# A 512x2048 by 2048x2048 product in seven block products instead of eight, at the end of a two-layer kernel

## The chip, the core and the metric

The kernel runs on one core of a Trainium2 chip. A core has a matrix engine (TensorE, PE in the profile), an elementwise engine (VectorE, DVE), an activation engine (ScalarE, ACT), a general engine (GpSimd, POOL) and a queue for transfers (SyncE, SP); ACT and POOL issue transfers too. Each engine works off its own list of instructions in order, and waits at an instruction until the semaphores it names have come. The metric is the device time of one execution in microseconds, lower is better. The kernel before took 2392.82 us, the median of three runs from 2391.46 to 2393.68 us.

## The reference

Two transformer-like layers on 512 tokens of width 2048, in float32. Only the end of the second layer matters here: `x` is 512x2048, `w_ple_gate` is 2048x2048, and `p @ w_ple` has long been computed and stored.

```python
x = x + merged @ w_out
x = x + jax.nn.sigmoid(x @ w_ple_gate) * (p @ w_ple)
return rms_norm_2(x, final_g)          # x * rsqrt(mean(x*x) + 1e-6) * final_g, by token
```

## The kernel before

**One stream of weights.** The whole kernel is one list, `spine`, of units. A unit is a block of weights of 512 KB (128 partitions by 1024 numbers, in the last group 256 KB) and the matmuls that use it. Float32 accuracy comes from three matmuls in the `fp32r` type: a value is split into `hi` (the value rounded to fp32r) and `lo` (the rest), and `mm3` adds hi*hi, hi*lo and lo*hi in PSUM. So every block of weights is loaded (`wraw`, SP's queue), copied by ACT to `whi` and subtracted by DVE to `wlo`; this is `split`. Buffers of these three kinds share a pool of NW = 10.

**The order of the work.** Nothing is scheduled later: the order in which `emit` writes instructions is the order on every engine. The loop at the end of `emit` takes unit after unit. Between the matmuls of unit i it calls `ahead`, which writes the loads up to unit i+4 (LD) and the splits up to unit i+3 (LS), and `sides.pump`, which writes steps of side work (`Sides`, generators that yield what they wait for) as far as the clocks of a simple model of the engines allow. What is needed at once is forced: `ahead(True)` splits the unit's own weights, and `sides.until` and `drain` run side work to a condition.

**The stage of the change.** `out2` (`ch_units("w_out_2", ...)`) makes the 16 row blocks of x transposed, 128 channels by 512 tokens each: 48 matmuls a block, then `after_o2` adds the old x and splits the sum into `x2h` and `x2l`, and `x2_gen` transposes it on PE (tile `px2`) and stores it by token (`x2t`). Then comes the gate product, in five column groups (`GATES`): three of 512 columns and two of 256. In a group of 512 columns a unit holds two of the 16 k blocks; its 24 matmuls serve four token blocks b of 128 tokens, in four PSUM banks. After the last unit of a group `after_gate` works on each token block: ACT takes tanh from PSUM, DVE does two `scalar_tensor_tensor` with the stored p @ w_ple (`plel`) and x (`x3`), ACT squares and sums, DVE multiplies by `final_g`. The last group keeps all its weights (`whole_units`) and runs token block by token block, each followed by `finish`: the mean square, an inverse square root by Newton steps of one column (`rsqrt1`), scaling and the store of 128 rows in four transfers.

## Time and profile before

| | us |
|---|---|
| runs (3) | 2391.46, 2392.82, 2393.68 |
| profiled execution | 2393.15 |
| its span, first to last instruction | 2391.4 |
| first matmul of the gate product | 2202.84 |
| last matmul of the gate product ends | about 2379.5 |
| TensorE busy in the span | 2360.1 |
| VectorE, ScalarE, GpSimd busy | 1478.4, 929.6, 251.1 |
| granted TensorE clock, mean | 0.999 |

The profile is one execution, and the prediction's rows are counted from its span's start. The busy time of PE is that of pipelined matmuls whose bars overlap: a 512-column matmul shows as 0.39 us, and one starts every 0.23 us. A row of the timeline gives the start, the time, the engine, the line of the kernel and `output<-inputs`, and in brackets the idle time before it and what ended it.

### The profile page before, as it was taken

The page shows a single profiled execution, that of the slowest core. Times are in us where ns is not written, and L with a number is a line of the kernel's source. Part 1 is how long each engine was busy: PE and PEld are TensorE (multiplying, and loading weights), DVE is VectorE, ACT ScalarE, POOL GpSimd, SP SyncE. Part 2 cuts the span into 40 slices and gives each one's busy share as a digit, 9 for nine tenths or more (in the row PEclk, how much of TensorE's full clock was granted, in tenths as well). Part 3 has the DMA queues.
Part 4 walks back from the last instruction along what each step waited for, and adds up shares of the span by engine and source line. Part 5 has one row for each costly group of instructions (what it writes and reads, how often), then busy time and mean ns, then how long its engine had stood idle before and what let it go on. Part 6 is the DMA issues. An engine that isn't in the chain of part 4 may idle for free.

```text
span 2391.4 us, 31046 instructions
## 1 busy us (share of the span) xinstructions
PE 2360.1 (99%) x11587; PEld 1985.0 (83%) x11587; DVE 1478.4 (62%) x2816; ACT 929.6 (39%) x1724; POOL 251.1 (11%) x376
## 2 busy tenths in 40 slices
PE   7999999999999999999999999999999999999998
PEld 5778889888888988888888888888888888888887
DVE  6787988788865367558878437777233444333336
ACT  5423265655533343335444234544233222222223
POOL 0000030332212001000000000000012100111201
PEclk9999999999999999999999999999999999999999
DMA  9986732333355333222222232222345533444633
GB/s 334 351 272 241 257 129 71 124 124 101 111 181 175 92 108 132 90 92 89 93 86 96 93 97 89 93 85 89 124 164 175 202 105 109 140 141 145 219 103 118
DMA packets 115783, 336.98 MB, mean 141 GB/s; under 512 B 15326, under 2 KB 15620, under 8 KB 115632
## 3 DMA queue, kind: packets, MB, share of 16 engines
q1 hardware_dynamic: 92016, 260.83, 32.8%
q0 software_dynamic: 22752, 73.02, 9.1%
q8 instruction: 91, 1.49, 0.3%
q10 hardware_dynamic: 864, 1.14, 0.1%
q14 instruction: 60, 0.49, 0.1%
HBM read 297.18 MB, written 37.75 MB: 140 GB/s over the span
## 4 chain that ended last, share of the span: by engine, by line
PE 85%; issue 6%; DVE 5%; ACT 2%; DMA 1%; POOL 1%; SPq 0%; POOLq 0%; DVEq 0%; ACTq 0%
PE pch L320 45%; PE ppan L320 14%; PE pp L320 9%; PE po L320 6%; PE psc L320 3%; PE pO L320 3%; PE pPT L324 2%; PE pearly L320 1%; DVE wlo L283 1%; PE pple L320 1%; PE pmod L534 1%; ACT whi L314 0%; DVE cA L283 0%; PE pada L320 0%; DMA wraw<-in_w_in_dram 0%
## 5 line engine op out<-in xcount | busy, mean ns | idle before, releaser
L283 DVE TENSOR_TENSOR wlo<-wraw,whi 128x1024 fp32r<-128x1024 f32 (+5 forms) x401 | 468.0, 1169 | 210.1 <-ACT whi L314 204.9
L314 ACT ACTIVATE whi<-wraw 128x1024 fp32r<-128x1024 f32 (+5 forms) x403 | 399.4, 1003 | 326.1 <-PE pch L320 115.1
L320 PE MATMUL pch<-h2h,whi 128*128 128x512 f32 x1216 | 483.3, 397 | 0.0
L320 PE MATMUL pch<-h2h,wlo 128*128 128x512 f32 x1216 | 474.9, 391 | 0.0
L320 PE MATMUL pch<-h2l,whi 128*128 128x512 f32 x1216 | 474.6, 390 | 0.0
L320 PEld LDWEIGHTS pch<-h2h,wlo 128*128 128x128 f32 x1216 | 228.2, 188 | 48.6
L320 PEld LDWEIGHTS pch<-h2h,whi 128*128 128x128 f32 x1216 | 228.6, 188 | 41.1
L320 PEld LDWEIGHTS pch<-h2l,whi 128*128 128x128 f32 x1216 | 228.8, 188 | 40.8
L314 ACT ACTIVATE P<-psc,sm 128x512 f32<-128x512 f32 (+3 forms) x160 | 83.6, 526 | 134.1 <-DVE sm L306 103.9
L320 PE MATMUL pp<-hh,whi 128*128 128x512 f32 x320 | 126.0, 394 | 0.2 <-DVE acc L283 0.2
L320 PE MATMUL pp<-hh,wlo 128*128 128x512 f32 x320 | 124.7, 390 | 0.0
L320 PE MATMUL pp<-hl,whi 128*128 128x512 f32 x320 | 124.6, 389 | 0.0
L320 PE MATMUL ppan<-whi,x2h 128*128 128x512 f32 (+1 forms) x320 | 111.0, 347 | 0.0
L320 PE MATMUL ppan<-whi,x2l 128*128 128x512 f32 (+1 forms) x320 | 110.9, 347 | 0.0
L320 PE MATMUL ppan<-wlo,x2h 128*128 128x512 f32 (+1 forms) x320 | 110.9, 347 | 0.0
L320 PE MATMUL pch<-mgh,whi 128*128 128x512 f32 x256 | 101.1, 395 | 0.0
L320 PE MATMUL pch<-mgh,wlo 128*128 128x512 f32 x256 | 99.9, 390 | 0.0
L320 PE MATMUL pch<-mgl,whi 128*128 128x512 f32 x256 | 99.7, 389 | 0.0
L320 PE MATMUL pch<-oh,whi 128*128 128x512 f32 x256 | 99.6, 389 | 0.0
L320 PE MATMUL pch<-ol,whi 128*128 128x512 f32 x256 | 99.6, 389 | 0.0
L320 PE MATMUL pch<-oh,wlo 128*128 128x512 f32 x256 | 99.6, 389 | 0.0
L314 ACT ACTIVATE PTh<-pPT 128x512 fp32r<-128x512 f32 (+1 forms) x120 | 59.5, 528 | 91.1 <-PE pPT L324 88.7
(500 smaller groups left out, 4635.0 us busy)
## 6 DMA issues: line engine op xcount, KB each, us to landing
wraw<-in_w_in_dram SPq DMA_DIRECT2D x199, 512.0 KB, 3.5
wada<-in_w_mod_dram SPq DMA_DIRECT2D x128, 256.0 KB, 5.4
wraw<-in_w_out_dram SPq DMA_DIRECT2D x64, 512.0 KB, 3.5
wgate<-in_w_gate_dram SPq DMA_DIRECT2D x64, 256.0 KB, 4.9
wraw<-in_w_ple_gate_dram SPq DMA_DIRECT2D x28, 512.0 KB, 3.5
sg<-mg POOLq DMA_DIRECT2D x32, 256.0 KB, 2.5
wraw<-in_w_up_b_dram SPq DMA_DIRECT2D x16, 512.0 KB, 3.5
sgl<-sg POOLq DMA_DIRECT2D x32, 256.0 KB, 6.1
```

Of the source, the lines that this page charges most:

```text
L283: V.tensor_tensor(o, a, b, op=op)
L314: A.activation(o, a, fn, **k)
L320: T.matmul(o, l, r, start=start, stop=stop_)
L324: T.transpose(o, a, i)
L534: T.matmul(acc[32 * q:32 * q + 32, :], cc[:, k, :], w.rearrange("p s n -> p (s n)"), start=first, stop=last_)
```

## The change

The gate product is computed in the Winograd form of Strassen's scheme. The weights are taken in two pairs of column blocks (p = 0 and 1) of 2 x 512 columns. For each pair the 2048 rows are halved (k blocks 0 to 7 and 8 to 15), the 512 tokens are halved, and the 2x2 by 2x2 block product is made of seven products instead of eight. Each product (`PROD`, in the order 1, 7, 6, 2, 5, 3, 4) takes eight k blocks, 256 tokens (j = 0, 1: two blocks of 128) and 512 columns: 48 matmuls in four units of 12.

- *Left factors* (`F`): sums of quarters of x, split into hi and lo, 7 x 8 tiles. `early_forms` makes those of products 1, 7 and 6 beside out2, whose row blocks now come in the order 0, 8, 1, 9, ...; `late_forms` makes those of 2, then 5 and 3 together, then 4, beside the products of pair 0. Pair 1 uses them again. x2h and x2l are gone.
- *Right factors*: the block sums of the weights are made in DRAM by 64 transfers on POOL's queue (`wsums`), 32 plain copies and 32 that add to their target, one to every second unit from unit 150 on. Products 7, 6, 5 and 4 load their weights from there.
- *Low parts by transfers* (`thin`): in pair 0, the second and fourth unit of every product are split without DVE. ACT writes hi, and then -hi into lo; a transfer on POOL's queue adds the raw weights to lo.
- *Results*: `after_prod` puts the seven products together with tensor_tensor steps on DVE, and runs the gating (`gated`) on whichever output blocks are complete. The last product of pair 1 holds its four units; its second half is run in two pieces of 256 columns.

The diff, cut to its core:

```diff
-GATES = ((0, 512), (512, 512), (1024, 512), (1536, 256), (1792, 256))
+THIN = True
+SUMS = 150
...
-    gate = [b for i, (c0, n) in enumerate(GATES)
-            for b in cut(rows(KT, (512 if i == len(GATES) - 1 else 1024) // n), c0, c0 + n, n)]
+    gate = cut(rows(KT, 2), 0, D, 512)
...
     def after_o2(m):
         def fn(ps):
-            x = xl.pop(m)
+            x = x2r[m] = xl.pop(m)
             tt(x, ps, x, OP.add)
-            x2h[m], x2l[m] = slot([128, 512], f"x2h{m}", F32R), slot([128, 512], f"x2l{m}", F32R)
-            split(x, x2h[m], x2l[m])
             sides.spawn(x2_gen(m, x))
+            if m >= 8:
+                sides.spawn(early_forms(m - 8))
         return fn
...
+    def quarters(k):
+        a, c = x2r[k], x2r[k + 8]
+        return a[:, 0:256], c[:, 0:256], a[:, 256:512], c[:, 256:512]
+    def form(q, k, x):
+        t = slot([128, 2, 256], "F" + q, F32R)
+        act(t[:, 0], x, AF.Copy)
+        yield [t]
+        tt(t[:, 1], x, f(t[:, 0]), OP.subtract)
+        F[q, k] = t
+    def early_forms(k):
+        x11, _, x21, x22 = quarters(k)
+        yield [x22]
+        yield from form("1", k, x11)
+        s = slot([128, 2, 256], "fs")
+        tt(s[:, 0], x11, x21, OP.subtract)
+        tt(s[:, 1], s[:, 0], x22, OP.add)
+        yield [s]
+        yield from form("7", k, s[:, 0])
+        yield from form("6", k, s[:, 1])
+    def late_forms():
+        for k in range(8):
+            yield
+            yield from form("2", k, quarters(k)[1])
+        for k in range(8):
+            x11, x12, x21, x22 = quarters(k)
+            yield
+            s = slot([128, 2, 256], "fs")
+            tt(s[:, 0], x21, x22, OP.subtract)
+            yield [s]
+            yield from form("5", k, s[:, 0])
+            tt(s[:, 1], x12, x11, OP.subtract)
+            tt(s[:, 1], s[:, 1], s[:, 0], OP.add)
+            yield [s]
+            yield from form("3", k, s[:, 1])
+            x2r.pop(k)
+        for k in range(8):
+            yield
+            yield from form("4", k, x2r[k + 8][:, 256:512])
+            x2r.pop(k + 8)
+    for n, m in enumerate(O2):
+        spine += ch_units("w_out_2", m * 128, 128, after_o2(m), out2_pre(n), KT, (mgh, mgl))
...
+    PROD = ("1", "7", "6", "2", "5", "3", "4")
+    PAIRS = (0, 1)
+    ws_d = {(p, n, u): dram(f"ws{p}{n}{u}", (128, 1024)) for p in PAIRS for n in ("x1", "x2", "x3", "y1") for u in range(4)}
+    def wblock(p, i, j, u):
+        k, c = 8 * i + 2 * u, (2 * p + j) * 512
+        return block("w_ple_gate_2", k, k + 2, (c, c + 512))
+    def wsums():
+        for p in PAIRS:
+            for step in range(8):
+                for u in range(4):
+                    d = {n: ws_d[p, n, u].rearrange("p (k n) -> p k n", k=2) for n in ("x1", "x2", "x3", "y1")}
+                    o, a = ((d["x1"], wblock(p, 0, 0, u)), (d["y1"], wblock(p, 1, 1, u)), (d["x1"], wblock(p, 0, 1, u)),
+                            (d["y1"], wblock(p, 0, 1, u)), (d["x2"], d["x1"]), (d["x2"], wblock(p, 1, 1, u)),
+                            (d["x3"], d["x2"]), (d["x3"], wblock(p, 1, 0, u)))[step]
+                    if step in (2, 3, 5, 7):
+                        G.dma_start(o, a, accum_op=OP.add, max_dma_last_dim=4096)
+                        clock.dma("G", o, a)
+                    else:
+                        dma("G", o, a)
+                    yield
+    def wsrc(p, q, u):
+        if q in "123":
+            return wblock(p, *{"1": (0, 0), "2": (1, 0), "3": (1, 1)}[q], u)
+        return ws_d[p, {"7": "y1", "6": "x2", "5": "x1", "4": "x3"}[q], u].rearrange("p (k n) -> p k n", k=2)
...
+    def gated(b, c, src, s=slice(0, 512), end=False):
+        x = x3[b, c][:, s]
+        t = slot([128, 512], "tgate")[:, s]
+        act(t, src, AF.Tanh, scale=0.5)
+        stt(t, t, 1.0, pl_[b, c][:, s], OP.add, OP.mult)
+        stt(x, t, 0.5, x, OP.mult, OP.add)
+        o = ssq[:, b, c:c + 1]
+        if end:
+            o = small("sqe")[:, 0:1]
+            stt(t, x, 1.0, x, OP.mult, OP.mult, accum_out=o)
+        else:
+            act(t, x, AF.Square, accum_out=o)
+        return o
...
+    def after_prod(p, q, j):
+        c = 2 * p
+        ps = acc[q, j] if q == "7" else acc.pop((q, j))
+        if q == "1":
+            t = tmp["1", j] = slot([128, 512], "q1")
+            act(t, ps, AF.Copy)
+        elif q == "6":
+            w = tmp["w", j] = slot([128, 512], "wq")
+            tt(w, ps, tmp["1", j], OP.subtract)
+        elif q == "2":
+            t = tmp.pop(("1", j))
+            tt(t, ps, t, OP.add)
+            gated(j, c, t)
+        elif q == "5":
+            e, t, w, p7 = slot([128, 512], "eq"), slot([128, 512], "c22"), tmp["w", j], acc.pop(("7", j))
+            tmp["e", j] = e
+            tt(e, ps, w, OP.add)
+            tt(t, e, p7, OP.subtract)
+            tt(w, p7, w, OP.subtract)
+            gated(2 + j, c + 1, t)
+        elif q == "3":
+            t = tmp.pop(("e", j))
+            tt(t, ps, t, OP.add)
+            gated(j, c + 1, t)
+        elif q == "4":
+            t = tmp.pop(("w", j))
+            tt(t, ps, t, OP.add)
+            gated(2 + j, c, t)
+        if p == 1:
+            if q in "253":
+                b, cc_ = {"2": (j, c), "5": (2 + j, c + 1), "3": (j, c + 1)}[q]
+                scaled(b, cc_)
+            if q == "3":
+                sides.spawn(finish(j, ()))
+            if q == "5":
+                sides.spawn(part_gen(2 + j))
...
+            if p == 0:
+                sides.until(lambda: (q, 2 * u + 1) in F)
+            if u:
+                return
+            if p == 0 and q == "1":
+                for _ in sums_:
+                    pass
+                sides.spawn(late_forms())
...
+        def mk(u):
+            def mmf(hi, lo):
+                if last_:
+                    held[u] = (hi, lo)
+                    if u == 3:
+                        yield from last_product(held)
+                    return
+                for j in range(2):
+                    if u == 0:
+                        acc[q, j] = bank("pg" + q)
+                    ps = acc[q, j]
+                    t = slice(j * 128, (j + 1) * 128)
+                    for kk in range(2):
+                        w = F[q, 2 * u + kk]
+                        mm3(ps, w[:, 0, t], w[:, 1, t], hi[:, kk, :], lo[:, kk, :], u == 0 and kk == 0,
+                            u == 3 and kk == 1)
+                        yield
+                    if u == 3:
+                        after_prod(p, q, j)
+                        yield
+                if p == 1:
+                    for kk in range(2):
+                        F.pop((q, 2 * u + kk))
+            return Unit(wsrc(p, q, u), (2, 512), mmf, pre=prod_pre(p, q, u),
+                        hold=(4 if u == 3 else 0) if last_ else 1, thin=THIN and p == 0 and u % 2 == 1)
+        return [mk(u) for u in range(4)]
+    def last_product(ws):
+        for j in range(2):
+            t = slice(j * 128, (j + 1) * 128)
+            sums = []
+            for s in (slice(0, 512),) if j == 0 else (slice(0, 256), slice(256, 512)):
+                ps = bank("pg4")[:, s]
+                for k in range(8):
+                    hi, lo = ws[k // 2]
+                    w = F["4", k]
+                    mm3(ps, w[:, 0, t], w[:, 1, t], hi[:, k % 2, s], lo[:, k % 2, s], k == 0, k == 7)
+                    yield
+                x = tmp["w", j][:, s]
+                tt(x, ps, x, OP.add)
+                sums.append(gated(2 + j, 2, x, s, s.stop == 512))
+            sides.spawn(finish(2 + j, sums))
...
+        for n, c in enumerate((2, 3, 1, 0)):
+            y = x3[b, c]
+            if sums and c == 2:
+                stt(y, y, r, pl_["fg", c], OP.mult, OP.mult)
+            elif n < 3:
                 act(y, y, AF.Identity, scale=r)
             else:
                 ts(y, y, r, None, OP.mult)
-            dma("QAQG"[c], out[0, b * 128:(b + 1) * 128, c * 512:(c + 1) * 512], x3[b, c])
+            dma("QAQG"[n], out[0, b * 128:(b + 1) * 128, c * 512:(c + 1) * 512], y)
...
+        elif u.thin:
+            act(u.hi, u.raw, AF.Copy)
+            act(u.lo, f(u.hi), AF.Copy, scale=-1.0)
+            G.dma_start(u.lo, u.raw, accum_op=OP.add, max_dma_last_dim=4096)
+            clock.dma("G", u.lo, u.raw)
...
+        if i >= SUMS and i % 2 == 0:
+            next(sums_, None)
```

What this makes of the engines' lists, at three places. First ACT, at the turn from product 7 to product 6 of pair 0 (numbers are those of the buffers; `whi`/`wlo` are the parts of a unit's weights, `F5` and `F3` left factors, `fs` their sums). Before, in the gate product, up to the first group's gating:

```order
L314 ACTIVATE whi_19309<-wraw_19273 128x1024
L314 ACTIVATE whi_19339<-wraw_19307 128x1024
L314 ACTIVATE whi_19369<-wraw_19337 128x1024
L314 ACTIVATE whi_19399<-wraw_19367 128x1024
L314 ACTIVATE tgate_19409<-ppan_19189 128x512
L314 ACTIVATE tgate_19409,ssq_209<-x3_19167 128x512
```

and now:

```order
L316 ACTIVATE whi_19423<-wraw_19388 128x1024
L316 ACTIVATE wlo_19424<-whi_19423 128x1024
L316 ACTIVATE whi_19438<-wraw_19409 128x1024
L316 ACTIVATE F5_19442<-fs_19428 128x256
L316 ACTIVATE whi_19467<-wraw_19433 128x1024
L316 ACTIVATE wlo_19468<-whi_19467 128x1024
L316 ACTIVATE F3_19472<-fs_19428 128x256
L316 ACTIVATE whi_19483<-wraw_19453 128x1024
```

Every second unit has two ACT instructions, and left factors stand between them; `wlo_19468` lies in the buffer of `wraw_19388`, which the transfer that completes `wlo_19424` reads.

Second DVE, in product 5 of pair 0, before its third unit's weights are used. The left factors were made in out2 before, one subtraction to a row block:

```order
L283 TENSOR_TENSOR x1l_18925<-pch_19009,x1l_18925 128x512
L283 TENSOR_TENSOR x2l14_19074<-x1l_18925,x2h14_19073 128x512
L283 TENSOR_TENSOR wlo_19080<-wraw_19042,whi_19079 128x1024
L283 TENSOR_TENSOR wlo_19119<-wraw_19077,whi_19118 128x1024
L283 TENSOR_TENSOR x1l_19001<-pch_19083,x1l_19001 128x512
```

Now, for k = 4 and 5 of products 5 and 3 (`x1l` are the quarters of x):

```order
L285 TENSOR_TENSOR wlo_19694<-wraw_19641,whi_19693 128x1024
L285 TENSOR_TENSOR F3_19672<-fs_19639,F3_19672 128x256
L285 TENSOR_TENSOR fs_19731<-x1l_18573,x1l_18645 128x256
L285 TENSOR_TENSOR F5_19733<-fs_19731,F5_19733 128x256
L285 TENSOR_TENSOR fs_19731<-x1l_18645,x1l_18573 128x256
L285 TENSOR_TENSOR fs_19731<-fs_19731 128x256
L285 TENSOR_TENSOR F3_19738<-fs_19731,F3_19738 128x256
L285 TENSOR_TENSOR fs_19741<-x1l_18729,x1l_18801 128x256
L285 TENSOR_TENSOR F5_19743<-fs_19741,F5_19743 128x256
L285 TENSOR_TENSOR fs_19741<-x1l_18801,x1l_18729 128x256
L285 TENSOR_TENSOR fs_19741<-fs_19741 128x256
L285 TENSOR_TENSOR wlo_19754<-wraw_19711,whi_19753 128x1024
```

Five DVE steps to a k block now stand behind the gating of product 2 and one unit's `wlo`, and the two `F` steps among them each read what ACT has just written from `fs`.

Third DVE, between product 5 of pair 1 and the third unit of product 3. The like place before, the gating of the second column group and the next unit's low part:

```order
L302 SCALAR_TENSOR_TENSOR x3_19451<-tgate_19693,x3_19451 128x512
L283 TENSOR_TENSOR x3_19451<-x3_19451,fg_19161 128x512
L302 SCALAR_TENSOR_TENSOR tgate_19705<-tgate_19705,plel_19456 128x512
L302 SCALAR_TENSOR_TENSOR x3_19455<-tgate_19705,x3_19455 128x512
L283 TENSOR_TENSOR x3_19455<-x3_19455,fg_19161 128x512
L302 SCALAR_TENSOR_TENSOR tgate_19717<-tgate_19717,plel_19460 128x512
L302 SCALAR_TENSOR_TENSOR x3_19459<-tgate_19717,x3_19459 128x512
L283 TENSOR_TENSOR x3_19459<-x3_19459,fg_19161 128x512
L302 SCALAR_TENSOR_TENSOR tgate_19729<-tgate_19729,plel_19464 128x512
L302 SCALAR_TENSOR_TENSOR x3_19463<-tgate_19729,x3_19463 128x512
L283 TENSOR_TENSOR x3_19463<-x3_19463,fg_19161 128x512
L283 TENSOR_TENSOR wlo_19770<-wraw_19681,whi_19769 128x1024
```

and now:

```order
L285 TENSOR_TENSOR c22_20462<-eq_20461,pg7_20137 128x512
L285 TENSOR_TENSOR wq_20276<-pg7_20137,wq_20276 128x512
L304 SCALAR_TENSOR_TENSOR tgate_20466<-tgate_20466,plel_20386 128x512
L304 SCALAR_TENSOR_TENSOR x3_20385<-tgate_20466,x3_20385 128x512
L285 TENSOR_TENSOR x3_20385<-x3_20385,fg_20049 128x512
L285 TENSOR_TENSOR eq_20478<-pg5_20406,wq_20284 128x512
L285 TENSOR_TENSOR c22_20479<-eq_20478,pg7_20144 128x512
L285 TENSOR_TENSOR wq_20284<-pg7_20144,wq_20284 128x512
L304 SCALAR_TENSOR_TENSOR tgate_20483<-tgate_20483,plel_20390 128x512
L304 SCALAR_TENSOR_TENSOR x3_20389<-tgate_20483,x3_20389 128x512
L285 TENSOR_TENSOR x3_20389<-x3_20389,fg_20049 128x512
L285 TENSOR_TENSOR wlo_20514<-wraw_20449,whi_20513 128x1024
```

Three more 512-column steps stand in each chain (`eq`, `c22`, `wq`), and two chains of six stand ahead of a unit's low part where four chains of three stood; the unit behind them has 12 matmuls where it had 24.

## Rows read from the trace of the kernel before

**Rows 1.** The page's first part: busy us, share of the span, instructions, by engine.

```profile
PE 2360.1 (99%) x11587; PEld 1985.0 (83%) x11587; DVE 1478.4 (62%) x2816; ACT 929.6 (39%) x1724; POOL 251.1 (11%) x376
```

**Rows 2.** Waits of TensorE over the whole span: us in total, times, longest.

```profile
PE pple L320 <- ACT whi L314: 9.4, 1, 9.4
PE psv L320 <- DVE wT L283: 1.6, 1, 1.6
```

**Rows 3.** The chain that ended last, from out2 into the gate product: start, us.

```profile
2201.44 0.70 DVE x1l L283
...
2202.19 0.66 PE px L324 x4
2202.84 126.53 PE ppan L320 x558
```

**Rows 4.** End of the timeline of TensorE: 256-column matmuls of the last group.

```profile
2379.11 0.28 PE L320 MATMUL ppan<-wlo,x2h 128*128 128x256 f32 x1
...
2379.23 0.28 PE L320 MATMUL ppan<-whi,x2l 128*128 128x256 f32 x1
```

**Rows 5.** Groups by line and shape, 2203 to 2392: busy us, mean ns.

```profile
L283 DVE TENSOR_TENSOR wlo<-wraw,whi 128x1024 fp32r<-128x1024 f32 x26 | 31.8, 1225 | 60.8 <-ACT whi L314 57.4 <-PE ppan L320 2.5 <-DVE wlo L283 0.4
L314 ACT ACTIVATE whi<-wraw 128x1024 fp32r<-128x1024 f32 x26 | 26.8, 1054 | 63.1 <-PE ppan L320 49.8 <-DMA wraw<-in_w_ple_gate_dram 10.2 <-ACT whi L314 1.9
...
L302 DVE SCALAR_TENSOR_TENSOR x<-tgate,x 128x512 f32<-128x512 f32 x12 | 8.3, 692 | 0.4
...
L314 ACT ACTIVATE tgate<-ppan 128x512 f32<-128x512 f32 x12 | 7.0, 584 | 15.8 <-PE ppan L320 15.8
...
L283 DVE TENSOR_TENSOR x<-x,fg 128x256 f32<-128x256 f32 x4 | 1.7, 426 | 2.3 <-ACT tgate L314 2.3
...
L314 ACT ACTIVATE tgate<-x 128x256 f32<-128x256 f32 x4 | 1.7, 418 | 4.0 <-DVE x L302 4.0
```

**Rows 6.** Timeline of DVE: gating of the third column group, then low parts.

```profile
2330.03 0.69 DVE L302 SCALAR_TENSOR_TENSOR tgate<-tgate,plel 128x512 f32<-128x512 f32 x1 [5.11 <-ACT tgate L314]
2330.76 0.69 DVE L302 SCALAR_TENSOR_TENSOR x<-tgate,x 128x512 f32<-128x512 f32 x1
2332.24 0.69 DVE L283 TENSOR_TENSOR x<-x,fg 128x512 f32<-128x512 f32 x1 [0.79 <-ACT tgate L314]
2332.84 0.68 DVE L302 SCALAR_TENSOR_TENSOR tgate<-tgate,plel 128x512 f32<-128x512 f32 x1
...
2340.66 0.69 DVE L283 TENSOR_TENSOR x<-x,fg 128x512 f32<-128x512 f32 x1 [0.79 <-ACT tgate L314]
2341.61 3.56 DVE L283 TENSOR_TENSOR wlo<-wraw,whi 128x1024 fp32r<-128x1024 f32 x4 [0.26 <-ACT whi L314]
```

**Rows 7.** DMA issues, 2000 to 2392: KB each, median us from issue to landing.

```profile
wraw<-in_w_ple_gate_dram SPq DMA_DIRECT2D x28, 512.0 KB, 3.5
...
plel<-ple POOLq DMA_DIRECT2D x12, 256.0 KB, 6.9
```

**Rows 8.** Stretches: length, busy us (instructions) by engine, PEclk, DMA share, GB/s.

```profile
60.00:100.00 40.00, 40.00 (x187) 29.95 (x187) 28.60 (x42) 19.93 (x31) 0.00 (x0) 1.00 1.00 360
...
2000.00:2203.00 203.00, 202.22 (x923) 167.10 (x922) 72.98 (x80) 53.32 (x71) 17.75 (x28) 1.00 0.43 130
```

**Rows 9.** The same for the stretch in which the transfers into DRAM would run.

```profile
860.00:1720.00 860.00, 857.95 (x4154) 712.04 (x4153) 576.48 (x1271) 352.05 (x686) 33.95 (x60) 1.00 0.29 95
```

**Rows 10.** Timeline of TensorE just after its one long wait.

```profile
11.21 0.63 PE L320 MATMUL pple<-whi,pTl 128*128 128x512 f32 x1
11.64 0.63 PE L320 MATMUL pple<-whi,pTh 128*128 128x512 f32 x1
...
15.48 0.51 PE L320 MATMUL pple<-whi,pTh 128*128 128x512 f32 x1
15.83 0.39 PE L320 MATMUL pple<-wlo,pTh 128*128 128x512 f32 x1
16.06 0.40 PE L320 MATMUL pple<-whi,pTl 128*128 128x512 f32 x1
```

**Rows 11.** Timeline of the end: Newton steps and the last store.

```profile
2381.98 1.31 DVE L302 SCALAR_TENSOR_TENSOR part<-part 128x1 f32<-128x1 f32 x6
...
2384.76 0.54 POOL L328 DMA_DIRECT2D out_dram<-x  x1 [5.22 <-DVE x L292]
```

More of the change, by code (lines that the diff above doesn't have):

```diff
@@ L237, with __init__ @@
 class Unit:
-    def __init__(self, src, shape, mm, pre=None, hold=1, half=False):
+    def __init__(self, src, shape, mm, pre=None, hold=1, half=False, thin=False):
         self.src, self.shape, self.mm, self.pre, self.hold, self.half = src, shape, mm, pre, hold, half
+        self.thin = thin
         self.raw = self.hi = self.lo = None
@@ L2114, in rsqrt1 @@
         return y
[L2116 to L2118 removed]
+    for p in PAIRS:
+        for q in PROD:
+            spine += prod_units(p, q)
     issued = {"dma": 0, "split": 0, "live": 0, "i": 0}
@@ L2180, in emit @@
     begin()
+    sums_ = wsums()
     for i, u in enumerate(spine):
```

107 lines of the change are left out of this document (47 added, 60 removed).

## The prediction

> **What bounds the kernel now.** I read the page's busy shares first. TensorE is busy for 2360.1 of the span's 2391.4 us [rows 1], so the reader should see a stream of matmuls with almost no holes. The list of its waits says the same: 9.4 us once, at the start, 1.6 us once, and nothing in the gate product [rows 2]. The chain that ended last enters the gate product through the last block of out2: x is added (2201.44), transposed on TensorE (2202.19), and from 2202.84 one chain of 558 matmuls takes 126.53 us, 0.2268 us each [rows 3]. The 256-column matmuls of the last groups start 0.12 us apart and the last ends at about 2379.5 [rows 4]. The groups give the price of one step on each engine [rows 5], the timeline the pace at which dependent steps follow each other [rows 6]. So fewer matmuls shorten the kernel one for one, as long as VectorE, ScalarE and the transfers keep up. That is the question: a unit had 24 matmuls (5.45 us) and now has 12 (12 x 0.2268 = 2.72 us), with the same split to be made for it.
>
> **What is saved.** Before, 576 matmuls of 512 columns and 384 of 256: 576 x 0.2268 + 384 x 0.12 = 176.7 us. Now 14 products of 48; the very last quarter (24 matmuls) is made as 48 of 256 columns: 648 x 0.2268 + 48 x 0.12 = 152.7. Saved 23.9 us. The first product needs left factors of row blocks 0 and 8, long made, so TensorE need not wait for the last block's add and split [rows 3]: of those 1.4 us some 0.4 (four transposes) remain. Saved in all 24.9 us.
>
> **Pair 1: no unknown price, but a queue.** Splits are written up to three units ahead; while the first matmuls of a product run, DVE has the first two units' low parts done at best, and the third unit's stands behind `after_prod` of the product before. Let T be the end of a product on TensorE; its j = 0 half was complete 12 x 0.1134 = 1.36 us before, and the third unit's low part is asked for at T + 2 x 2.72 + 0.23 = T + 5.67. The chains on DVE go at 0.73 us for a dependent step (2330.03 to 2330.76) and 0.60 for an independent one (2332.24 to 2332.84); between the second step and the `final_g` step lies ScalarE's square, 0.76 us [rows 6]; tanh takes 0.6, `whi` 1.05, `wlo` 1.23 [rows 5]. ScalarE cannot start `whi` before it is through the second half's square.
> - Behind products 2 and 4 one chain is add 0.72, tanh 0.6, two steps 1.46, square 0.76, last 0.6, some 4.14 with `final_g` and 2.78 to the square without. Product 1 (pair 1), third unit: squares done at T + 5.0, `whi` 6.05, `wlo` 7.3, asked 5.67: wait 1.6. Product 5, third unit: 2 x 4.14 - 1.36 = 6.9, `whi` beside it, `wlo` T + 8.6: wait 2.9.
> - Behind product 5 the chain has eq and c22 more, 4.85: 2 x 4.85 - 1.36 = T + 8.3, `whi` 8.8, `wlo` 10.0: product 3 waits 4.4.
> - Product 4 holds four units and runs by token block; its third unit's low part stands behind both chains of product 3, the part sums (1.1) and the other low parts: done at T + 24.8, asked 18.25: wait 6.5.
> In sum 15.4. Before, the same gating of four blocks held DVE for 11.3 us (2330.03 to 2341.35), and the low parts came only then [rows 6], without a wait, because three units were 16.3 us ahead; now they are 8.2.
>
> **Pair 0: left factors.** `late_forms` for k = 4 to 7 of products 5 and 3 run while product 5 does: per k five 256-column steps of DVE (0.43) and two of ScalarE (0.42) that alternate [rows 5], 5 x 0.43 + 2 x 0.42 = 3.0 us and more where a low part goes between, against 1.36 us of matmuls per k. Following the order block by block, product 5 waits 3.3, 2.2, 1.4 and 2.2 (9.1), product 3's third unit, behind gating and factors, 3.1, and product 4, whose fourth factor stands behind product 3's gating, 3.9. In sum 16.1.
>
> **Pair 0: transfers that add.** No row shows one. A plain weight load of 512 KB lands 3.5 us after its issue, a 256 KB load on POOL's queue after 6.9 [rows 7]; at full DMA load 360 GB/s were moved, 512 KB in 1.46 us [rows 8]. The transfer reads two streams and writes one. Lower bound: as the plain load, 3.5. Upper: 8 (6.9 and one more pass). I take 3.5 + 1.46 = 5.0, nearest to the weight load, which has its size and shape. Then, for a thin unit, hi copy 1.05, -hi copy 1.05, landing 5.0, 0.1 to the matmul: 7.2 from the start of the hi copy, against 5.44 of two units. The hi copy itself is late where its buffer is the raw weights of an earlier thin unit, which that unit's transfer still reads. By order of the list: product 1, second unit, 1.3 and fourth 1.5; product 7, 3.4 (behind the q1 copies) and 1.7; the next three 0.66 each (only the -hi copy waits, 6.1 against 5.44); product 2's fourth 2.8, product 3's 3.1, product 4's 1.1. In sum 15.6; with 3.5 us about 5, with 8 about 35.
>
> One rule of the Trainium skill speaks against my price ("DMA: Bandwidth & Descriptors", section "Anatomy of one DMA — SWDGE (gpsimd) path"): such a transfer costs about 2.0 us and its bytes at 436 GB/s. By that, an estimate, 512 KB land in 3.2 us and the sum would be some 10 us lower; counted twice for the two streams, 4.4 us and 5 lower. The POOL row, 6.9 us for 256 KB, lies above it.
>
> **Tail.** Before, 2391.4 - 2379.5 = 11.9 us lie between the last matmul and the end. Now DVE still has the `finish` of token blocks 0 and 1 when the last matmuls run (Newton steps 0.22 us each, 1.31 for six; part chains and scalings [rows 11]), 2.6 each, then block 2 (3.5), block 3 in two halves (1.8 + 2.2) and the two last part chains (3.6 and, past the last matmul, 3.4); with 6.6 from the last store's issue to the end (2384.76 to 2391.4) and the scaling ahead of it the end comes 19.3 after the last matmul: +7.4. Bounds: 0 if all that hides, 11.
>
> **Costed at nothing.** The 64 transfers in DRAM go out from unit 150 on, about one in 10.9 us from 860 to 1720 us. There the DMA engines are 29% busy with 95 GB/s [rows 9], and weights are loaded four units (21.8 us) ahead of a landing of 3.5. Each adds 0.5 to 1 MB in 10.9 us, some 90 GB/s. Their cover is this lead; a landing delayed by 20 us would cost its excess. The earlier factors beside out2 add about 6 us to DVE, which is busy 73.0 of 203 us there, ACT 53.3 [rows 8]. The other order of out2's blocks costs nothing: the same units.
>
> **Sum.** 2393.15 (profiled, 1.75 of it outside the span and within 0.4 of the median) - 24.9 + 15.4 + 16.1 + 15.6 + 7.4 = 2422.8: forecast 2423 us.
>
> **Rivals.**
> 1. *The clock.* The one long wait of before, 9.4 us, is followed by 512-column matmuls 0.43 us apart: ten from 11.21 to 15.48, 4.27 us instead of 2.27, and two more ahead of them, so some 2.4 us lost before the pace is 0.23 [rows 2, 10]. Over the whole span the granted clock is 0.999, so the wait of 1.6 us brought no such stretch. If each of the six waits over 3 us above (3.3, 3.1, 3.9, 3.4, 4.4, 6.5) is followed by a like loss, 6 x 2.4 = 14 us come on top: 2437. For it: those rows. Against: 9.4 us was the start, with nothing before it; 3 to 6.5 lies between the two rows. The Trainium skill ("TensorE: Matmul & The Clock Gate", section "HAM oscillation — how this bites in real kernels") tells of a kernel that fell to the low clock anew after every wait for a transfer, which would be this rival. Chance 0.15.
> 2. *The adding transfer lands late*, 8 to 12 us, because reading, adding and writing are done in turn or POOL's queue is slow (6.9 for half the bytes): thin units then set pair 0's pace; seven products with two of them, some 2 to 4 us more each: 2450 and above. Chance 0.10.
> 3. *The lead swallows the waits* (the other side): the low parts do not in fact stand behind the gating, because gating on ScalarE and DVE of the two halves overlaps better than one chain after the other. The place is the third unit of the products of pair 1; the longest work ahead of a low part there is 10.0 us against a lead of 8.2, so a fifth less in each chain and landings of 3.5 would end nearly all waits but the factors': 2393.15 - 24.9 + 7.4 = 2375.7 with none, and faster as long as the waits sum to less than 17.5. Against: the order on DVE shows twelve steps in one row. Chance 0.08, and 0.03 that the sum ends at no change.
> 4. *The DRAM sums hold up weight loads* between 860 and 1720: each stall of 5 us, ten of them, 2470. Against: the share of 0.29. Chance 0.03, within the upper tail.
>
> **How the numbers follow.** My forecast with its own terms: 0.61, by itself 2408 to 2436: the transfer bounds give -10 to +20, the tail -7 to +4, and both ends together are unlikely. Adding half of the clock's case above and some of rival 3 below, 2406 to 2448 should hold 8 of 10. About 0.2% (4.8 us) is what a measurement tells from no change. Faster: rival 3, 0.08. Within 0.2%: 0.03. Slower: the rest, 0.89.
>
> **What would show it.** In the profile after, TensorE's waits in the gate stage should name, in pair 0, `wlo` from the adding transfer and `F5`/`F3` from ACT and DVE, in pair 1 `whi` and `wlo` behind gating, 4 to 7 us at products 3 and 4. Product 5 of pair 0 should take some 20 us instead of 10.9. The adding transfers should land after about 5 us. The tail should be near 19 us, and no wait should appear from 860 to 1720. Wrong would be: waits below 17 us in sum (rival 3); matmuls 0.43 us apart behind the waits (rival 1); landings over 8 (rival 2).

## The result: 2446.74 us, slower by 2.3%

The changed kernel took 2446.74 us, the median of four runs from 2445.12 to 2449.18, against 2392.82 before: the ratio is 1.0227, with a 95% interval of 1.0209 to 1.0244. It lies inside the forecast's range and on its side, but 24 us above its value and close to the range's upper end of 2448. The profiled execution took 2449.18 us with a span of 2447.3, against 2393.15 and 2391.4.

TensorE's share and the granted clock in 40 slices, from the page of the profile after, answer to [rows 1]:

```profile
PE 2364.3 (97%) x11323; PEld 1973.0 (81%) x11323; DVE 1528.9 (62%) x2914; ACT 985.7 (40%) x1799; POOL 303.0 (12%) x446
...
PEclk9999999999999999999999999999999999999897
```

TensorE has 264 matmuls fewer and is busy for longer. The clock row says why: it is below nine tenths only in two of the last three slices, in the gate product. The waits of TensorE after ([rows 2] had none in this stage), us in total, times, longest:

```profile
PE pg L322 <- DMA wlo<-wraw: 22.1, 10, 5.0
PE pg L322 <- ACT whi L316: 11.4, 4, 4.7
...
PE pg L322 <- ACT F L316: 5.8, 3, 2.8
PE pg L322 <- DVE F L285: 3.3, 1, 3.3
PE pg L322 <- DVE wlo L285: 2.7, 4, 0.8
...
PE phid L322 <- DVE cAl L285: 1.4, 2, 0.8
```

The five rows on `pg` sum to 45.3 us. The forecast's three sums were 47.1, in the same three kinds: adding transfers (22.1 here), left factors (9.1), and in pair 1 `whi` and `wlo` behind gating (14.2).

A piece of TensorE's timeline around one of them, product 3 of pair 1 (start, time, then the idle time before and its end; [rows 3, 4 and 10] are the like rows of before):

```profile
2203.84 0.39 PE L322 MATMUL pg<-whi,F 128*128 128x512 f32 x1
...
2397.73 0.39 PE L322 MATMUL pg<-whi,F 128*128 128x512 f32 x1
2401.57 0.50 PE L322 MATMUL pg<-whi,F 128*128 128x512 f32 x1 [3.45 <-ACT whi L316]
2402.83 0.79 PE L322 MATMUL pg<-wlo,F 128*128 128x512 f32 x1 [0.76 <-DVE wlo L285]
2403.42 1.05 PE L322 MATMUL pg<-whi,F 128*128 128x512 f32 x2
2404.28 0.63 PE L322 MATMUL pg<-wlo,F 128*128 128x512 f32 x1
2404.70 1.05 PE L322 MATMUL pg<-whi,F 128*128 128x512 f32 x2
2405.56 0.63 PE L322 MATMUL pg<-wlo,F 128*128 128x512 f32 x1
2405.98 0.76 PE L322 MATMUL pg<-whi,F 128*128 128x512 f32 x2
...
2429.06 0.28 PE L322 MATMUL pg<-whi,F 128*128 128x256 f32 x1
```

A hole of 3.45 and 0.76 us, then from 2402.83 to 2405.98 seven matmuls in 3.15 us instead of 1.59: the pace of half clock, 0.43 us apart, as after the start's wait [rows 10]. The clock granted from 2402.8 to 2406.0 was 0.51 of full, the lower of its two levels. The same list has eleven such stretches. The stretches of the stage show it too (columns as in [rows 8], the eighth figure is the clock):

```profile
860.00:1720.00 860.00, 856.72 (x4142) 710.90 (x4141) 575.56 (x1270) 351.62 (x686) 77.31 (x122) 1.00 0.46 133
...
2200.00:2300.00 100.00, 75.74 (x281) 58.39 (x280) 45.37 (x83) 48.15 (x73) 15.94 (x23) 0.87 0.75 205
2300.00:2400.00 100.00, 86.47 (x342) 68.10 (x341) 58.91 (x73) 42.13 (x62) 15.56 (x27) 0.93 0.73 234
```

The account of the stage from 2203.84 to the last matmul's end at 2429.3, 225.5 us: 152.7 of matmuls, 0.4 of transposes, 45.3 of waits, 20.3 lost at half clock (for each matmul in the slow stretches its distance to the next less 0.2268), and 7.0 of restarts (behind a hole the next matmuls come 0.1 to 0.3 us late, 22 times); these parts sum to 225.7. Before it was 176.9: by TensorE's timeline the first `ppan` matmul starts at 2202.60, and 2202.84 is only where the chain of [rows 3] enters. The tail went from 11.9 to 18.0, and the stage began 1.2 later. Together 48.6 + 6.1 + 1.2 = 55.9, the whole difference of the spans.

### The profile page after: what moved, and what is told of

It reads as the page before. It is cut to its first block, busy times and chain, and to the rows that moved or that the text cites. A ratio compares the mean times of both kernels' runs of the same rounds, so it can differ in the third digit from the quotient of the medians.

```text
span 2447.3 us, 30887 instructions
## 1 busy us (share of the span) xinstructions
PE 2364.3 (97%) x11323; PEld 1973.0 (81%) x11323; DVE 1528.9 (62%) x2914; ACT 985.7 (40%) x1799; POOL 303.0 (12%) x446
## 5 line engine op out<-in xcount | busy, mean ns | idle before, releaser
L285 DVE TENSOR_TENSOR wlo<-wraw,whi 128x1024 fp32r<-128x1024 f32 (+5 forms) x407 | 481.1, 1183 | 219.1 <-ACT whi L316 203.5
L316 ACT ACTIVATE whi<-wraw 128x1024 fp32r<-128x1024 f32 (+5 forms) x423 | 424.4, 1013 | 339.8 <-PE pch L322 119.8
L322 PEld LDWEIGHTS pch<-h2h,wlo 128*128 128x128 f32 x1216 | 228.5, 188 | 48.6
L322 PE MATMUL pg<-whi,F 128*128 128x512 f32 (+1 forms) x464 | 155.9, 418 | 20.5 <-ACT whi L316 11.4
L322 PEld LDWEIGHTS pg<-whi,F 128*128 128x128 f32 x464 | 95.9, 209 | 44.1 <-ACT whi L316 13.1
L322 PE MATMUL pg<-wlo,F 128*128 128x512 f32 (+1 forms) x232 | 98.8, 426 | 24.8 <-DMA wlo<-wraw 22.1
```

Source lines behind the costliest of these rows:

```text
L285: V.tensor_tensor(o, a, b, op=op)
L316: A.activation(o, a, fn, **k)
L322: T.matmul(o, l, r, start=start, stop=stop_)
```

## The experiments

Each kernel's time is a median over its runs (e4 and e8 have two, e7 one). The ratio is to the kernel before, run again beside each set (medians 2392.08 to 2392.75); the changed kernel has 1.0227. Waits, half clock and tails are those of the one profiled execution of each. In the edits `...` marks what is left out.

**e1: low parts of pair 0 by GpSimd instead of transfers.**

```diff
-            act(u.lo, f(u.hi), AF.Copy, scale=-1.0)
-            G.dma_start(u.lo, u.raw, accum_op=OP.add, max_dma_last_dim=4096)
-            clock.dma("G", u.lo, u.raw)
+            gtt(u.lo, u.raw, f(u.hi), OP.subtract)
```

> One edit: the 14 thin units of pair 0 get their low part from one GpSimd subtraction of 1024 columns (2.4 to 3.0 us in the two rows at the start of the trace) instead of the -hi copy on ScalarE and the adding transfer, which landed after 4.6 to 8.0 us, median 5.7. Theory: 22.1 us of TensorE's waits in the changed kernel are for these transfers; with hi copy 1.05 and 2.7 us on GpSimd the low part is ready 3.8 us after the copy begins, under the 5.4 us of two units, so some 18 of the 22 go, and with them some 5 stretches at half clock of about 2 us: 2447 - 18 - 10 = about 2419, the waits on F and on whi/wlo of pair 1 unchanged (some 23 us). Rival: the transfers only show the wait that ScalarE and VectorE would cause anyway (hi copies behind squares, F steps); then the waits turn up on whi, GpSimd or F, and the time stays within 5 us of 2447.

2425.82 us, 1.0141 (1.0126 to 1.0156). TensorE's waits in the gate product:

```profile
PE pg L322 <- ACT whi L316: 17.1, 7, 5.2
PE pg L322 <- DVE wlo L285: 6.4, 8, 1.2
PE pg L322 <- DVE F L285: 5.7, 3, 4.6
PE pg L322 <- ACT F L316: 3.0, 2, 1.5
PE pg L322 <- POOL wlo L289: 2.6, 2, 2.0
```

The waits for transfers are gone, but those on `whi`, F and VectorE's `wlo` grew from 23.2 to 32.2 us. With GpSimd's own 2.6 they are 34.8 in all, where the theory left 27: three quarters of the expected gain, and a part of the rival. e5 shows one reason.

**e2: holes of pair 1 filled.**

```diff
+                if p == 1 and u == 2 and q in "153":
+                    warm(acc[q, 0], F[q, 4], {"1": 9, "5": 12, "3": 18}[q])
...
+                    if j == 0 and k == 4:
+                        warm(ps, w, 22)
...
+    zf = cp.tile([128, 128], F32R, name="zf")
+    act(zf, ones, AF.Copy, scale=0.0)
...
+    def warm(ps, w, n):
+        for _ in range(n):
+            T.matmul(ps, zf, w, start=False, stop=False)
```

> One edit: in pair 1, ahead of the third unit of products 1, 5, 3 and 4, TensorE gets 9, 12, 18 and 22 matmuls of 512 columns with a zero left side into the bank that is being summed, about as long (0.2268 us each: 2.0, 2.7, 4.1, 5.0 us) as the holes that the changed kernel's trace has there (1.27+0.76, 2.00+0.76, 3.45+0.76, 4.72+0.47). They add 61 matmuls, 13.8 us of work, and compute nothing. Theory of the clock: the slow stretch after each of these holes (matmuls 0.43 us apart for some 2 us) comes from TensorE having stood idle; filled, the holes cost the same time but the clock stays full, so the time falls by about 4 x 2 = 8 us to about 2439, with no 0.43 us pace after 2330 in the trace. Rival: the slow pace has another cause (what the other engines do to the memories at that moment, or the kind of matmul); then the pace stays at 0.43 there and the time is 2447 or up to 14 more.

2445.04 us, 1.0221 (1.0204 to 1.0238). The same place as above, product 3 of pair 1, in its timeline:

```profile
2394.69 3.56 PE L2211 MATMUL pg<-F,zf 128*128 128x512 f32 x15
2399.40 0.50 PE L322 MATMUL pg<-whi,F 128*128 128x512 f32 x1 [1.15 <-ACT whi L316]
2400.66 0.50 PE L322 MATMUL pg<-wlo,F 128*128 128x512 f32 x1 [0.76 <-DVE wlo L285]
2401.00 0.62 PE L322 MATMUL pg<-whi,F 128*128 128x512 f32 x2
2401.45 0.40 PE L322 MATMUL pg<-wlo,F 128*128 128x512 f32 x1
```

The pace behind is 0.23 us. From 2330 to 2425 us the changed kernel and then e2 were granted this clock (the eighth figure):

```profile
2330.00:2425.00 95.00, 80.82 (x323) 64.11 (x322) 65.05 (x100) 40.12 (x56) 9.09 (x17) 0.91 0.55 191
```

```profile
2330.00:2425.00 95.00, 90.49 (x417) 74.47 (x415) 65.81 (x101) 42.28 (x58) 9.11 (x17) 1.00 0.58 203
```

The slow stretches of pair 1 are gone, and those of the whole stage fall from 20.3 to 13.0 us: it is the idle TensorE that lowers the clock, not the kind of matmul or the neighbours. The Trainium skill ("TensorE: Matmul & The Clock Gate", "HAM oscillation — how this bites in real kernels") tells of a kernel whose engine fell to the low clock anew after every wait for a transfer. The runs agree in kind, with 1.6 us lost in the example above, but not in the "every": 22 holes of the changed kernel brought eleven stretches.

The time fell by 1.7 us, not 8, which the intervals don't tell from nothing. The last matmul started at 2423.2, only 5.9 us earlier: the 61 matmuls take 13.8 us and replaced 11.2 us of pair 1's waits. The tail then grew from 18.0 to 20.2, since VectorE's work behind it came 3.7 us earlier and not 5.9. So part of what the clock gave back went into filling too much and part into VectorE's list, which neither theory had.

**e3: gating as side work.**

```diff
-            gated(j, c, t)
+            sides.spawn(gate_side(p, j, c, t))
...
+    def gate_side(p, b, c, src):
+        yield [src]
+        x, t = x3[b, c], slot([128, 512], "tgate")
+        act(t, src, AF.Tanh, scale=0.5)
+        yield [t]
+        stt(t, t, 1.0, pl_[b, c], OP.add, OP.mult)
+        stt(x, t, 0.5, x, OP.mult, OP.add)
+        yield [x]
+        act(t, x, AF.Square, accum_out=ssq[:, b, c:c + 1])
+        if p == 1:
+            yield [t]
+            scaled(b, c)
...
```

> One edit: the gating of an output block (tanh, two steps, square, final_g) is side work, taken in pieces between the units when the model of the engines has time, instead of written as one run at the end of a product; adds from PSUM stay where they were. Low parts of the third units then stand ahead of the gating on VectorE, and whi ahead of the squares on ScalarE. Theory (the queue): the waits of pair 1 (1.27+0.76, 2.00+0.76, 3.45+0.76, 4.72+0.47, in all 14.2 us) fall to 3 or less, and with them 3 to 4 stretches at half clock (8 us); pair 0's waits lose 2 to 4 of their 31; the tail may grow by up to 3 since the gating of the last blocks is later: about 2447 - 11 - 8 - 3 + 3 = 2428. Rival: VectorE's and ScalarE's total work sets the pace (not the order), so the waits move to the next unit and the time stays within 4 us of 2447.

2430.24 us, 1.0156 (1.014 to 1.0171). All of TensorE's waits in the gate product:

```profile
PE pg L322 <- DMA wlo<-wraw: 26.7, 9, 5.1
PE pg L322 <- ACT F L316: 3.4, 3, 2.0
```

Pair 1 has none left. The last matmul starts at 2402.8, 26 us earlier; the tail grew to 26.2, which takes 8 of them back. The queue of the prediction is shown: the same steps in another order, and the 14.2 us are gone.

**e4: late left factors left out.**

```diff
+    MADE = {"1": "1", "7": "7", "6": "6", "2": "1", "5": "7", "3": "7", "4": "6"}
...
-                sides.spawn(late_forms())
...
-                        w = F[q, 2 * u + kk]
+                        w = F[MADE[q], 2 * u + kk]
...
```

> Leaves out the late left factors: products 2, 5, 3 and 4 use the tiles of products 1, 7, 7 and 6, so 64 VectorE steps and 32 ScalarE copies of 256 columns are not made and the output is another. Theory: product 5's and 3's waits for F (2.78, 1.98, 1.03, 3.26: 9.1 us) go with the two or three slow stretches behind them (6 us), and the transfers' waits in products 2, 5 and 3 (5.04, 4.15, 2.98) shrink to about 2 each because their copies no longer stand behind F steps on ScalarE: 2447 - 9 - 6 - 6 = about 2426. Rival: the transfers' waits are the landing alone and take over what F leaves, about 2440.

2441.18 us, 1.0204 (1.0183 to 1.0224): the rival. (By the traces 56 VectorE steps are left out, not 64.) The waits for F are gone, but those for the transfers rise from 22.1 to 26.1, and all waits fall by 3.5 only. In product 5 one wait of 4.95 us for a transfer stands where the three for F stood: two things were late at the same place, and taking one away uncovers the other.

**e5: e1 and e3 together.**

> The edits of e1 (low parts of pair 0's thin units by GpSimd) and e3 (gating as side work) together. e1 left waits of 21.5 us in pair 0 and 13.3 in pair 1 with 8.7 us of slow pace; e3 left none in pair 1, but 26.7 for the adding transfers and 3.4 for F in pair 0, and a tail of 26 us. Theory (two separate queues): both gains add up, waits of about 8 us in all, one slow stretch of 2: first matmul 2203.5 + 152.7 + 8 + 2 + 4 of restarts = last matmul at 2370, tail 26, 1.9 outside: about 2398. Rival: VectorE's total work is the bound by then (low parts, F, gating, sums): the waits come back on DVE wlo and F as in e1's pair 0 (some 18 us), about 2412.

2401.63 us, 1.0038 (1.0024 to 1.0052), between the two and nearer to the theory. Waits fell to 12.3 us. Part of VectorE's time went into steps that stood still, as its timeline and GpSimd's of the same moment show:

```profile
2236.28 0.42 DVE L285 TENSOR_TENSOR F<-fs,F 128x256 fp32r<-128x256 f32 x1
2236.62 2.61 DVE L285 TENSOR_TENSOR fs<-x1l 128x256 f32<-128x256 f32 x1
2239.26 0.43 DVE L285 TENSOR_TENSOR fs<-fs 128x256 f32<-128x256 f32 x1
```

```profile
2236.50 2.44 POOL L289 TENSOR_TENSOR wlo<-wraw,whi 128x1024 fp32r<-128x1024 f32 x1 [4.84 <-DVE wlo L285]
```

The VectorE step of 0.42 us took 2.61 and ended 0.3 us after GpSimd's subtraction. Over pair 0 the group of these steps has a mean of 936 ns here and 419 ns without GpSimd's subtractions (e10):

```profile
L285 DVE TENSOR_TENSOR fs<-x1l 128x256 f32<-128x256 f32 x17 | 15.9, 936 | 0.0
```

```profile
L285 DVE TENSOR_TENSOR fs<-x1l 128x256 f32<-128x256 f32 x17 | 7.1, 419 | 0.0
```

The Trainium skill has the rule ("SBUF — State Buffer", "Who interferes with whom"): a VectorE instruction with two SBUF inputs contends with a GpSimd instruction that reads SBUF. The trace agrees: in e6 a step with one input in PSUM kept its 0.69 us beside a subtraction (next).

**e6: GpSimd in pair 1 too.**

Against e5, cut to the changed ends of lines:

```diff
...
-thin=THIN and p == 0 and u % 2 == 1
+thin=THIN and u % 2 == 1
...
-            if j == 1:
-                sides.until(lambda: {0, 1} <= fin)
...
+                sides.until(lambda: {0, 1} <= fin)
```

> e5 with every second unit of pair 1 split by GpSimd too (14 more subtractions of 2.7 us), and with blocks 0 and 1 finished before the last product's first half is added. VectorE has 17 us less in pair 1, so gating and sums come earlier and the tail should lose what e3's gained: theory 2398 - 6 = about 2392, last matmul as in e5. Rival: GpSimd's queue, in which the loads of plel and x stand and wait for buffers, holds up low parts in pair 1 (each such wait 3 to 10 us): 2405 or more.

2407.12 us, 1.0063 (1.0048 to 1.0078): 5.5 us slower than e5. Of the expected tail gain of 6 us 2.6 came (from 25.6 to 23.0), but the last matmul started at 2381.2 instead of 2372.9, with 4.5 us of waits in pair 1, where e5 has none. In time this is the rival. In place it is not: GpSimd's subtractions were released by `whi` or `wlo`, not by loads, and the collision of e5 turns up in pair 1. GpSimd's and VectorE's timelines:

```profile
2350.14 2.58 POOL L289 TENSOR_TENSOR wlo<-wraw,whi 128x1024 fp32r<-128x1024 f32 x1 [3.91 <-ACT whi L316]
...
2358.88 5.72 POOL L289 TENSOR_TENSOR wlo<-wraw,whi 128x1024 fp32r<-128x1024 f32 x2 [4.08 <-ACT whi L316]
```

```profile
2350.63 0.69 DVE L285 TENSOR_TENSOR eq<-pg,wq 128x512 f32<-128x512 f32 x1 [0.19 <-PE pg L322]
...
2360.33 2.01 DVE L285 TENSOR_TENSOR wlo<-wraw,whi 128x1024 fp32r<-128x1024 f32 x1 [1.37 <-ACT whi L316]
2362.27 2.88 DVE L285 TENSOR_TENSOR x<-x,fg 128x512 f32<-128x512 f32 x1
```

The step that reads PSUM (`eq`) is not held; `wlo` (1.22 us otherwise) and the `final_g` step (0.69 otherwise) are. How many of the 5.5 us the collision makes was not tried apart.

**e7: the transfers copy instead of add.**

```diff
-            G.dma_start(u.lo, u.raw, accum_op=OP.add, max_dma_last_dim=4096)
+            G.dma_start(u.lo, u.raw, max_dma_last_dim=4096)
```

> The changed kernel with the 14 transfers into the low parts of pair 0 copying the raw weights instead of adding them, so the output is another: same bytes read from the raw buffer and written, without reading the target. If the addition makes the landing long, it falls from 5.7 us (median) to about 3.5, the plain load's, the waits for them from 22 to about 8 and the time to about 2425. If the landing is that of any transfer on this queue with this shape, it stays above 5 and the time at 2447.

2434.59 us in its one run. The landing of these 14 transfers, first in the changed kernel, then copied:

```profile
DMA to landing us min/median/max: 4.6/5.7/8.0
```

```profile
DMA to landing us min/median/max: 2.9/3.6/5.7
```

The add lands 2.1 us later than the copy, and without it the waits for the transfers fall from 22.1 to 9.8 us. The waits on `whi`, `wlo` and F take 2.6 of these 12.3 us back, and 16 of the 20.3 us at half clock stay, so the time lies between the two expectations.

**e8: no sums in DRAM.**

```diff
...
-        return ws_d[p, {"7": "y1", "6": "x2", "5": "x1", "4": "x3"}[q], u].rearrange("p (k n) -> p k n", k=2)
+        i, j = {"1": (0, 0), "2": (1, 0), "3": (1, 1), "7": (0, 1), "6": (1, 1), "5": (0, 1), "4": (1, 0)}[q]
+        return wblock(p, i, j, u)
...
-        if i >= SUMS and i % 2 == 0:
-            next(sums_, None)
```

> Leaves out the 64 transfers that make block sums of the weights in DRAM; products 7, 6, 5 and 4 read plain blocks of the weights, so the output is another. I costed the transfers at nothing. Then the first matmul of the gate product stays within 0.7 us of 2203.8 and the time within 3 us of 2447. Rival: they delay weights somewhere from 860 to 1720 or, by their buffers in DRAM, the loads of the gate product (landing 4.0 to 5.6 us there, 3.5 before): then the start moves by 1 us or more and the time falls by more than 4.

2444.11 us (two runs, 2441.29 and 2446.93), 1.0215 (1.0195 to 1.0235). The time can't tell it, since the two runs lie 5.6 apart. In the profiled one the gate product starts at 2197.85, 6.0 us earlier than in the changed kernel, but 3.1 of them stand already at 851.7, where one of the 64 transfers has gone out. The nine kernels with these sums, whose lists are nearly the same up to the gate product, start it anywhere from 2200.8 to 2205.1, so the start can't tell it either. The stretch between can. From 900 to 1000 us, the changed kernel and then e8:

```profile
900.00:950.00 50.00, 48.25 (x241) 40.49 (x240) 38.03 (x79) 17.29 (x29) 7.74 (x13) 0.97 0.41 127
950.00:1000.00 50.00, 48.56 (x256) 40.37 (x255) 33.29 (x74) 19.55 (x38) 10.86 (x15) 1.00 0.81 217
```

```profile
900.00:950.00 50.00, 48.35 (x251) 40.61 (x250) 37.99 (x80) 18.34 (x34) 9.12 (x14) 1.00 0.41 132
950.00:1000.00 50.00, 49.64 (x261) 41.46 (x260) 30.49 (x70) 19.22 (x35) 0.58 (x1) 1.00 0.28 88
```

With the sums TensorE waits 1.0 us more for `cAl`. The clock of 0.97 belongs to a slow stretch behind the wait for `wT` at 913.97, which is as long in e8 (1.7 us) without one. The sums don't make this stretch: e10, whose sums begin only at 950.7, has it too:

```profile
900.00:950.00 50.00, 48.20 (x241) 40.40 (x241) 36.26 (x77) 17.31 (x29) 8.47 (x13) 0.97 0.39 124
```

And e3, e4, e5, e6 and e11 have the same sums without it. From the first to the last product of `h2` (tile `pch`, 851.7 to 1848.2 in the changed kernel) it takes 993.7 us before and 993.6 in e8, 995.1 to 995.5 in these five, and 996.5 to 997.0 in the four with the stretch (the changed kernel, e1, e2 and e7). So the sums cost 1.5 to 1.9 us, and the stretch, which comes in some kernels and not in others, 1.4 more.

**e9: e5, sums later, a shorter end.**

```diff
-SUMS = 150
+SUMS = 172
...
+                if j == 0:
+                    sides.until(lambda: ng[0] == 4 and ng[1] == 4)
...
-        r = rsqrt1(ms)
+        r = rsqrt1(ms) if b == 3 else rsqrt1_pool(ms)
...
-            dma("QAQG"[n], out[0, b * 128:(b + 1) * 128, c * 512:(c + 1) * 512], y)
+            dma("QAQG"[n] if b == 3 else "QAQQ"[n], out[0, b * 128:(b + 1) * 128, c * 512:(c + 1) * 512], y)
...
```

The stores of blocks 0 to 2 also leave GpSimd's queue for SyncE's, which the expectation doesn't name.

> e5 with three edits. (1) The DRAM sums begin at unit 172 instead of 150, past the stage from 910 to 985 us where the kernels with them lose 1.6 to 3.4 us against the one without: the start of the gate product comes some 2.5 us earlier. (2) The Newton steps of blocks 0, 1 and 2 run on GpSimd, some 6 us less VectorE work at the end. (3) The gating of blocks 0 and 1 is written ahead of the last product's first add, so that the square of block 1 no longer stands behind six scalings on ScalarE. Theory (VectorE's work sets the tail of 26 us): tail 21 to 22, time 2401.6 - 2.5 - 4.5 = about 2395. Rival: small steps on GpSimd take longer than on VectorE, and scalings on ScalarE and VectorE wait for them in order: tail 26 or more, about 2399.

2396.6 us, 1.0016 (1.0007 to 1.0024): 1.6 above the theory and 2.4 below the rival. The tail is 22.7 us; the gate product starts 1.3 us earlier than in e5, not 2.5.

**e10: e9 with every low part on VectorE.**

```diff
-THIN = True
+THIN = False
```

> e9 with all low parts on VectorE, none on GpSimd or by transfers. In e5's trace a VectorE step of two SBUF operands that meets a GpSimd subtraction takes 1.9 to 2.6 us instead of 0.42 or 1.22 (2236.62, 2250.90, 2263.29, 2265.44). Theory (VectorE and GpSimd share the way to SBUF in such steps): 14 subtractions cost VectorE about 2 us each in stalls, more than the 1.14 us that it takes to do one itself; without them VectorE has some 10 us more in pair 0, waits there fall from 12 us to 5 or less, and the time by 5 to 9, to about 2388. Rival (VectorE's count of steps is the bound): 14 x 1.14 = 16 us more work in pair 0, waits come back on wlo and F, 2400 to 2405.

2382.39 us, 0.9956 (0.9943 to 0.997): 0.4% faster than the kernel before, a small gain but clear of the noise. This is the only wait of TensorE in the gate product:

```profile
PE pg L322 <- ACT F L316: 1.9, 1, 1.9
```

From the first matmul (2201.08) to the end of the last (2357.4) it takes 156.4 us, 3.7 over the bare matmuls and 20.5 less than before: the seven products keep what they promise once nothing stands in their way. The tail of 23.1 us, 11.2 longer than before, takes more than half of that back. And the theory of e5 is borne out: in e5's pair 0 thirteen steps that write F, `fs` or `wlo` stood still for some 24 us in all, and here none does.

**e11: the changed kernel, only `THIN = False`.** The edit is e10's line, in the changed kernel.

> The changed kernel with one part of the change undone: pair 0's thin units are split like all others, low part on VectorE (14 x 1.22 us), no copies of -hi and no adding transfers. Gating stays as it was, in one run at the end of a product. Theory from e10, which had 1.9 us of waits in the whole stage with all low parts on VectorE: the transfers cost more than they saved; the 22.1 us of waits for them and the slow stretches behind them (10 us) go, some 5 to 10 us of waits for wlo and F come in their place because gating stands ahead of them: about 2425. Rival: without gating as side work VectorE is short in pair 0, and the waits for wlo and F grow by 20 us or more: 2440 or above.

2415.89 us, 1.01 (1.0085 to 1.0115): one part of the change undone, and 31 us are back. TensorE's waits in the gate product:

```profile
PE pg L322 <- ACT whi L316: 16.4, 6, 4.7
PE pg L322 <- DVE F L285: 4.0, 1, 4.0
PE pg L322 <- DVE wlo L285: 4.0, 6, 0.8
PE pg L322 <- ACT F L316: 1.5, 1, 1.5
```

25.9 us are left, 13.7 of them in pair 1 (14.2 in the changed kernel), and 11.8 us of half clock. The theory's mechanism held, 9 us stronger than its size: the waits on `whi`, `wlo` and F rose by 2.7 us, not by 5 to 10.

**e12: another order at the end of e10.**

```diff
-            if j == 1:
-                sides.until(lambda: {0, 1} <= fin)
...
-                    sides.until(lambda: ng[0] == 4 and ng[1] == 4)
+                    sides.until(lambda: {0, 1} <= rsd)
...
-        r = rsqrt1(ms) if b == 3 else rsqrt1_pool(ms)
+        r = rsqrt1(ms) if b in (1, 3) else rsqrt1_pool(ms)
+        rsd.add(b)
...
```

> e10 with another order at the end: the Newton steps of block 1 back on VectorE and ahead of the last product's first add (on GpSimd they ended 3.2 us late at 2362.8), and the scalings of blocks 0 and 1 no longer forced ahead of the last product's second half, so that tanh does not wait 2.0 us behind them on ScalarE. Theory: the tail of 23 us loses 2 to 4, about 2380. Rival: the eight scalings now stand at the end of ScalarE's list and the last stores wait for them; 2382 or more.

2384.23 us, 0.9963 (0.9949 to 0.9977): not told apart from e10. VectorE ended at 2370.4 instead of 2373.3, but the scalings then stood at the end of ScalarE's list, to 2375.3, and the tail is 24.9 us: the rival.

## Why the prediction was right, and where it was short

- **Saved matmuls, -24.9.** Right: 152.7 us of matmuls are in the account, and e10 gets down to 156.4. The 1.0 at the end of out2 came too: from the last product of `h2` to the first of the gate it was 357.0 us before and 355.6 now, with 0.4 of transposes moved into the stage. Yet the stage began 1.2 later and not 1.0 earlier, see the DRAM sums.
- **Pair 1, 15.4 us forecast.** Measured 14.2, by place 2.0, 2.8, 4.2 and 5.2 against 1.6, 2.9, 4.4 and 6.5. The mechanism, low parts behind gating in one list, is shown by e3.
- **Left factors, 16.1.** Measured 9.1: product 5 waited 2.8, 2.0 and 1.0 instead of 9.1 in all, product 3 not at all for F instead of 3.1, and product 4 3.3 instead of 3.9. Why the factors were less late than the chains made them was not tried apart. That product 5 took 20.0 us as forecast is luck: 5.8 of waits and 3.3 of half clock and restarts in place of 9.1 of waits.
- **Adding transfers, 15.6.** Its own places add up to 16.9. Measured 22.1; the landing was 5.7 where I took 5.0, and up to 8.0. The upper end of 8 was a good bound. That all waits together came to 45.3 against 47.1 is in part luck as well: the transfers' were 6.5 too low and the factors' 7.0 too high. An estimate by the fit of the Trainium skill ("DMA: Bandwidth & Descriptors", "Anatomy of one DMA — SWDGE (gpsimd) path"), 3.2 us for 512 KB, would have made the sum lower still. By it e7's copies, with 3.6, come near and the adding transfers don't; the measurement decides.
- **Tail, +7.4.** Measured 6.1.
- **DRAM sums, 0.** Measured 1.5 to 1.9 us, in the stage from 910 to 985 us where TensorE already waited for VectorE (1.6 us [rows 2], which the sign "no wait from 860 to 1720" passed over). The mean DMA share of 29% [rows 9] says little of single stretches: from 950 to 1000 us the share is 0.81 with the sums and 0.28 without. The 64 transfers went out one in 14.8 us and not in 10.9, and added 38 GB/s in the mean, not 90 ([rows 9] had 95 GB/s, now it is 133). How the sums delay `cAl` was not tried. Another 1.4 us of the late start came from the slow stretch at 914, which is not theirs.
- **The step that failed** is the price of a wait. The sum took each wait at its length, and put the clock in a rival of 0.15, as six like losses of 2.4 us on top. That rival came true and larger: 20.3 us at half clock in eleven stretches, and 7.0 of restarts that stood nowhere. It counted the holes over 3 us (its own lists have seven, since 3.1 stands twice); one of 1.94 us and several pairs such as 1.27 and 0.76 brought the slow pace as well. 2422.8 + 20.3 + 7.0 + 2.2 (the late start) - 1.8 (waits) - 1.3 (tail) = 2449.2, the time of the profiled execution. By its own terms the forecast ended at 2436; the range held the result because half of the clock's case had been added to it.
- **What the prediction did not ask** is what VectorE would make of the same low parts. e11 shows it: with them on VectorE the waits for transfers have no successor of their size, and the time falls by 31 us.

## What to carry to other kernels

When half the matmuls of a unit go, the lead shrinks by half in time though not in units: ask what stands ahead of the next operand in each engine's list, and put work that nobody waits for (here gating) behind it. Price a hole in TensorE's stream with what follows it, the slow pace and the restart, and expect to get that back only where no other engine sets the end. Before an engine is relieved by a transfer or by GpSimd, compare the whole latency of the new way, and what it holds meanwhile, with the few us of the step it replaces.
